# The first norm of a hybrid trunk step: its modulation by quarters of a channel, two column blocks ahead on rows 0 and 1, statistics in two parts

## The chip, the cores and the metric

One core of one Trainium2 chip runs the whole program. The metric is device time in microseconds, the median of three runs. The core has TensorE (PE, and PEld for its weight loads), VectorE (DVE), ScalarE (ACT), GpSimd (POOL) and SyncE (SP), whose queue issues most of the transfers.

## What is computed

One layer of a trunk on 640 tokens (128 of a prompt, 512 latent) of width 1024 in float32: a half-step SwiGLU feed-forward, a mixer, a second feed-forward, a last norm. The change touches only the first norm and the first products of the first feed-forward:

```python
mod = jax.nn.silu(cond) @ w_mod + b_mod              # cond: c or c_ctx
sh1, sc1, g1, shm, scm, gm, sh2, sc2, g2 = jnp.split(mod, N_MOD, axis=-1)
h = modulate(rmsnorm(x, norm_g[0]), sh1, sc1)        # h * (1 + sc1) + sh1
x = x + 0.5 * g1[:, None, :] * swiglu(h, ffn1_w1, ffn1_w2)
```

## The kernel before

Everything is kept transposed: 8 row tiles k of 128 features, 640 tokens in two halves h of 320. A product of float32 is made of three TensorE products of rounded parts (`three`, lines 245 to 247: hi by hi, lo by hi, hi by lo), 320 columns each; "a three" below is these. `split` (L75, L79) makes hi on ACT and lo on DVE, of weights (128x512, `wh`, `wl`) and of activations (128x320, `H..h`, `H..l`). The order of each engine's queue is that in which the program emits its instructions.

The stretch before the first full block goes so. SP issues ten loads of x (`x_load`), then the eight loads of channels SC1 and SH1 for rows 0 to 3 (the "upper" half, 512 KB each, `mod_load`: 2 KB packets), five into the ring `wr` and three into tiles `early`, then the weights of column blocks 0 and 1 for rows 0 to 3 (`two(0)`) and of block 2, then the eight loads for rows 4 to 7 ("low" units). Meanwhile `consts_in` makes silu of the conditioning (`cm`), `first(ch)` transposes a chunk of 128 tokens on PE, squares it on ACT with a sum along the row, and copies it out of PSUM (6 copies on DVE, 2 on ACT), `first_rows` makes the reciprocal norms of all five chunks (Sqrt, reciprocal, six diagonal matrices `dg`), and `rows_fn` spreads them by products with ones into two PSUM tiles (`N["rb", h]`). `scale_x` (L800) multiplies x by them.

A unit (L570) multiplies `cm` by one loaded tile: in `mod_half(.., wide=True)` two row tiles by 512 columns, so that four units make half a channel. Then `rows_` (L577) copies its PSUM rows, `turn` (L582) transposes them, and `put_` (L587, L589) sums four groups, adds the bias and writes `modT`. `gain` (L718, L719) makes the scale. `modulate` (L808 on ACT, L810 on DVE) applies scale and shift, and `first_put` splits the result into `H11` (h = 0, rows 0 to 3), `HT4` (h = 1, rows 0 to 3), `H21` and `H22` (rows 4 to 7).

`first_head` holds the first products: three column blocks t, halves h, rows k. For each h and each k of 0 to 3 it multiplies all three blocks, and between these it emits, by the table `then`, the low units, their rows, turns and puts, the remaining `scale_x` (`later`: eight of them), and the splits of the second half of the weights (`uncap`). Then `lower` modulates and splits rows 4 to 7, and k = 4 to 7 follow. PSUM comes from two pools of four banks, `big()` (`ps`) and `aux()` (`ax`).

POOL's queue loads channel G1 into the two tiles `mg` (`mod_own`); its first pair of loads waits for nothing but its place in the queue.

## Time and profile before

| what | us |
|---|---|
| median of 3 runs | 1672.75 (1672.16 to 1673.14) |
| the profiled execution, its own time | 1673.05 |
| its span, first to last instruction | 1671.3 |
| TensorE busy in the span | 1652.6 |
| VectorE busy | 1259.8 |
| ScalarE busy | 792.5 |

TensorE is busy in 99% of the span, and the granted clock is 1.00 in every slice. The page's 40 slices are 41.8 us each: only the first has TensorE at less than nine tenths, and the last one. A line of a timeline is one group of equal instructions of an engine, with its start, how long from the first start to the last end, and, in brackets, how long the engine had been idle and what ended that. A group's length is longer than the engine's step from one instruction to the next, because instructions overlap.

### The profile page before, as it was taken

What the parts mean: (1) busy time and instruction counts of PE and PEld (TensorE: products, weight loads), DVE (VectorE), ACT (ScalarE), POOL (GpSimd) and SP (SyncE); (2) the same over time, 40 slices, a digit from 0 to 9 for tenths busy, and PEclk for the clock granted to TensorE, in tenths of its full rate; (3) what the DMA queues carried; (4) which work ended last, traced back from release to release, by engine and by line L of the source; (5) the groups of instructions that cost most, each with busy time, mean ns of one, the idle gap of its engine ahead of it and who ended that gap; (6) DMA issues with size and microseconds to landing.
All of it is one profiled execution on the core that took longest, in us unless ns stands there. A gap on an engine that the chain in (4) does not pass through costs nothing.

```text
span 1671.3 us, 29257 instructions
## 1 busy us (share of the span) xinstructions
PE 1652.6 (99%) x11172; PEld 1607.3 (96%) x11172; DVE 1259.8 (75%) x2676; ACT 792.5 (47%) x1723; POOL 169.0 (10%) x251
## 2 busy tenths in 40 slices
PE   8999999999999999999999999999999999999998
PEld 4989999999999999999999999999999999999997
DVE  5867786887778778788897898779587467476576
ACT  5542452542565555455561455632375245254253
POOL 2010000000030321221121221011100000000002
PEclk9999999999999999999999999999999999999999
DMA  9344343343352533343258333457341322233221
GB/s 341 91 152 127 89 126 115 114 117 99 112 164 75 133 101 89 81 113 76 84 180 262 107 89 82 112 175 213 101 127 46 106 77 70 82 89 89 76 76 64
DMA packets 270972, 193.07 MB, mean 116 GB/s; under 512 B 8963, under 2 KB 247930, under 8 KB 270832
## 3 DMA queue, kind: packets, MB, share of 16 engines
q1 hardware_dynamic: 261248, 158.42, 32.6%
q0 software_dynamic: 9552, 32.77, 6.9%
q8 instruction: 88, 1.44, 0.4%
q14 instruction: 52, 0.43, 0.1%
q10 hardware_dynamic: 32, 0.01, 0.0%
HBM read 175.87 MB, written 15.31 MB: 114 GB/s over the span
## 4 chain that ended last, share of the span: by engine, by line
PE 93%; DMA 2%; ACT 2%; DVE 2%; issue 1%; SPq 0%; POOL 0%; ACTq 0%; DVEq 0%; POOLq 0%
PE ps L245 28%; PE ps L246 28%; PE ps L247 28%; PE ax L1460 2%; PE ax L1491 2%; PE ax L1463 1%; PE ax L570 1%; DMA wr<-in_w_mod_dram 1%; PE ax L1437 1%; DMA early<-in_w_mod_dram 0%; DMA wh<-in_x_sample_dram 0%; PE ax L661 0%; ACT Uh L808 0%; DMA wr<-in_w_ml_out_dram 0%; DVE wl L79 0%
## 5 line engine op out<-in xcount | busy, mean ns | idle before, releaser
L79 DVE TENSOR_TENSOR wl<-wr,wh 128x512 fp32r<-128x512 f32 (+1 forms) x408 | 267.1, 669 | 80.8 <-ACT wh L75 78.8
L75 ACT CAST wh<-wr 128x512 fp32r<-128x512 f32 (+1 forms) x410 | 239.1, 595 | 155.7 <-PE ps L246 136.6
L79 DVE TENSOR_TENSOR wl<-ws,wh 128x512 fp32r<-128x512 f32 x288 | 202.5, 703 | 44.9 <-ACT wh L75 44.1
L75 ACT CAST wh<-ws 128x512 fp32r<-128x512 f32 x288 | 176.1, 620 | 103.9 <-DVE ws L218 62.4
L245 PE MATMUL ps<-Uh,wh 128*128 128x320 f32 x704 | 218.8, 311 | 0.0
L246 PE MATMUL ps<-Ul,wh 128*128 128x320 f32 x704 | 217.2, 309 | 0.0
L247 PE MATMUL ps<-Uh,wl 128*128 128x320 f32 x704 | 217.1, 308 | 0.0
L889 DVE SCALAR_TENSOR_TENSOR x<-ps,modT,x 128x128 f32<-128x128 f32 (+2 forms) x216 | 82.8, 434 | 113.9 <-PE ps L247 113.8
L245 PEld LDWEIGHTS ps<-Uh,wh 128*128 128x128 f32 x704 | 132.1, 188 | 1.2 <-issue 0.8
L246 PEld LDWEIGHTS ps<-Ul,wh 128*128 128x128 f32 x704 | 132.1, 188 | 0.2 <-DVE Ul L79 0.2
L247 PEld LDWEIGHTS ps<-Uh,wl 128*128 128x128 f32 x704 | 132.1, 188 | 0.0
L245 PE MATMUL ps<-H11h,wh 128*128 128x320 f32 x384 | 121.1, 315 | 0.0
L245 PE MATMUL ps<-HT4h,wh 128*128 128x320 f32 x384 | 120.9, 315 | 0.0
L245 PE MATMUL ps<-H21h,wh 128*128 128x320 f32 x384 | 120.3, 313 | 0.4 <-ACT H21h L75 0.4
L246 PE MATMUL ps<-H11l,wh 128*128 128x320 f32 x384 | 118.8, 309 | 0.1
L246 PE MATMUL ps<-H21l,wh 128*128 128x320 f32 x384 | 118.7, 309 | 0.1
L247 PE MATMUL ps<-HT4h,wl 128*128 128x320 f32 x384 | 118.6, 309 | 0.0
L247 PE MATMUL ps<-H11h,wl 128*128 128x320 f32 x384 | 118.6, 309 | 0.0
L246 PE MATMUL ps<-HT4l,wh 128*128 128x320 f32 x384 | 118.6, 309 | 0.0
L247 PE MATMUL ps<-H21h,wl 128*128 128x320 f32 x384 | 118.4, 308 | 0.0
L245 PE MATMUL ps<-H22h,wh 128*128 128x320 f32 x352 | 110.2, 313 | 0.0
L246 PE MATMUL ps<-H22l,wh 128*128 128x320 f32 x352 | 108.9, 309 | 0.2
(411 smaller groups left out, 4490.3 us busy)
## 6 DMA issues: line engine op xcount, KB each, us to landing
wr<-in_ffn_w_dram SPq DMA_DIRECT2D x86, 512.0 KB, 3.9
wr<-in_w_in_dram SPq DMA_DIRECT2D x72, 512.0 KB, 3.9
wr<-in_w_mod_dram SPq DMA_DIRECT2D x56, 512.0 KB, 4.3
wr<-in_ffn_w_dram SPq DMA_DIRECT2D x48, 384.0 KB, 3.5
wr<-in_ffn_w_dram SPq DMA_DIRECT2D x20, 256.0 KB, 3.3
mg<-in_w_mod_dram POOLq DMA_DIRECT2D x8, 512.0 KB, 5.3
early<-in_w_mod_dram SPq DMA_DIRECT2D x8, 512.0 KB, 9.4
wr<-in_w_ml_out_dram SPq DMA_DIRECT2D x8, 512.0 KB, 4.9
```

Of the source, the lines that this page charges most:

```text
L75: A.copy(hi, raw)
L79: V.tensor_sub(lo, raw, f32(hi))
L245: PE.matmul(ps, hi[:, ws], ah, start=start, stop=False, skip_group_check=True)
L246: PE.matmul(ps, hi[:, ws], al, start=False, stop=False, skip_group_check=True)
L247: PE.matmul(ps, lo[:, ws], ah, start=False, stop=stop, skip_group_check=True)
L570: PE.matmul(S["p"][g, c:c + n], cm[:, k, :], w[:, n * j:n * j + n], start=(k < 4), stop=(k >= 4), skip_group_check=True, tile_position=(0, ...
L889: V.scalar_tensor_tensor(X[m][:, o + a:o + b], ps[:, a:b], modT[:, g, m, cd:cd + 1], X[m][:, o + a:o + b], op0=OP.mult, op1=OP.add)
L1437: PE.matmul(p[:, :P], S["k", dt][:, sl], S["q", dt][:, sl], start=(dt == 0), stop=(dt == 1))
L1460: PE.matmul(p2[:, :DH + 1], S["q", dt][:, sl], S["C"][d][:, dt, :], start=(dt == 0), stop=(dt == 1))
L1463: PE.matmul(p1[:, :DH + 1], S["p", ch][:, d, :], PO["vt"][:, ch, :], start=True, stop=True)
L1491: PE.matmul(p[:, :DH + 1], kw[:, dt * P:(dt + 1) * P], PO["vt"][:, ch, :], start=True, stop=True)
```

## The change

- The upper units come as quarters of a channel (`mod_quarters`): a load is four row tiles by 256 columns (`quarter_load`, 1 KB packets), two units make two row tiles of one channel, and rows, turn and put are done for each quarter. The order is SC1 and SH1 for rows 0 and 1, then SC1 and SH1 for rows 2 and 3. All eight have tiles `early`; the low units come three in the ring (`RING`) and five in `early` tiles again.
- On SP the weights of blocks 0 and 1 are issued behind the first four quarters, block 2 behind the other four, then low units 0 to 2 and 3 to 6; low unit 7 is issued after the first weights of the second half (`two(4)`), which are issued as `two(0)` is split.
- Blocks 0 and 1 multiply rows 0 and 1 of both halves first; then follow the units of the second four quarters, block 2 on rows 0 and 1, and the rest in a new order (`products`, `go`).
- x's statistics come in two parts (`first_rows(0)` after three chunks, `first_rows(1)` after five), and the spread rows lie in `big()` tiles. `scale_x` of rows 2 and 3 moves into `first_head`, behind the splits of rows 0 and 1.
- A Sqrt of a constant stands first on ACT; the silu of `consts_in` comes behind both Sqrt of the statistics. ACT makes one of the eight copies of a chunk out of PSUM (chunks 0 to 2) or none, where it made two.
- POOL copies a column of `modT` (the last shift of SH1) into each `mg` tile ahead of its first load, which so waits for it.

```diff
--- before.py
+++ after.py
@@ -590,6 +590,43 @@
         loads = [(mod_load if wide else quarter_load)(ch, half, i) for i in range(4)]
         return [(loads[i], unit_(i)) for i in range(4)], [rows_, turn, put_]
+    def mod_quarters(ch, half):
+        S = {}
+        def unit_(i):
+            q = i // 2
+            def emit(w):
+                if i % 2 == 0:
+                    S["p", q] = aux()
+                for j in range(4):
+                    g = slice(32 * j, 32 * j + 32)
+                    PE.matmul(S["p", q][g, :256], cm[:, 4 * (i % 2) + j, :], w[:, 256 * j:256 * j + 256],
+                              start=(i % 2 == 0), stop=(i % 2 == 1), skip_group_check=True, tile_position=(0, g.start))
+            return emit
+        def steps(q):
+            def rows_():
+                S["r", q] = t3()
+                (A.copy if ch == SH1 else V.tensor_copy)(S["r", q][:, :256], S["p", q][:, :256])
+            def turn():
+                S["c", q] = aux()
+                for j in range(2):
+                    PE.transpose(S["c", q][:, j * P:j * P + P], S["r", q][:, j * P:j * P + P], ident)
+            def put_():
+                k0 = 4 * half + 2 * q
+                o = modT[:, ch, k0:k0 + 2, :]
+                b0 = ch * KT + k0
+                V.tensor_reduce(o, S["c", q][:, :256].rearrange("p (j g r) -> p j r g", j=2, g=4)[:, :, 0:2, :],
+                                axis=mybir.AxisListType.X, op=OP.add)
+                V.tensor_add(o, o, bmT[:, b0:b0 + 2, None].to_broadcast([P, 2, 2]))
+            return [rows_, turn, put_]
+        return [(quarter_load(ch, half, i), unit_(i)) for i in range(4)], [steps(0), steps(1)]
     def mod_own(ch):
@@ -602,6 +639,9 @@
         def load(*ii):
             for i in ii:
                 tiles[i] = PO["mg"].tile([P, 1024], F32, name="mg", bufs=2)
+                if i < 2:
+                    G.tensor_copy(tiles[i][:, 0:1], modT[:, SH1, KT - 1, 0:1])
                 us[i][0](tiles[i])
         def two(v, *more):
@@ -786,8 +826,8 @@
             out.append((dg, c1 - c0, dst))
         return out
-    def spread(dgs):
-        p = aux()
+    def spread(dgs, p=None):
+        p = p or aux()
         for dg, n, dst in dgs:
             PE.matmul(p[:, dst:dst + n], ones, dg[:, :n], start=True, stop=True)
         return p
@@ -981,16 +1021,20 @@
                     PE.transpose(p[:, k * P:(k + 1) * P], XI[ch, q][:, k * P:(k + 1) * P], ident)
                 A.activation(scr, XI[ch, q], AF.Square, accum_out=ssq[:, ch, q:q + 1])
                 for k in range(4):
-                    (A.copy if k == 3 else V.tensor_copy)(X[4 * q + k][:, sl], p[:, k * P:(k + 1) * P])
-            V.tensor_add(ss[:, ch:ch + 1], ssq[:, ch, 0:1], ssq[:, ch, 1:2])
+                    (A.copy if k == 3 and q == 1 and ch < 3 else V.tensor_copy)(X[4 * q + k][:, sl], p[:, k * P:(k + 1) * P])
         return f
-    def first_rows():
-        A.activation(ss, ss, AF.Sqrt, scale=1.0 / D, bias=eps)
-        V.reciprocal(ss, ss)
-        r = lambda ch: ss[:, ch:ch + 1]
-        N["dg", 0] = diags([(r(0), 0, P, 0), (r(1), 0, P, P), (r(2), 0, 64, 256)])
-        N["dg", 1] = diags([(r(2), 64, P, 0), (r(3), 0, P, 64), (r(4), 0, P, 192)])
+    def first_rows(h):
+        def f():
+            a, b = ((0, 3), (3, NCH))[h]
+            V.tensor_add(ss[:, a:b], ssq[:, a:b, 0], ssq[:, a:b, 1])
+            A.activation(ss[:, a:b], ss[:, a:b], AF.Sqrt, scale=1.0 / D, bias=eps)
+            V.reciprocal(ss[:, a:b], ss[:, a:b])
+            r = lambda ch: ss[:, ch:ch + 1]
+            N["dg", h] = diags([(r(2), 64, P, 0), (r(3), 0, P, 64), (r(4), 0, P, 192)] if h else
+                               [(r(0), 0, P, 0), (r(1), 0, P, P), (r(2), 0, 64, 256)])
+        return f
     def first_scale(h, k):
         return lambda: scale_x(h, k, N["rb", h])
@@ -1011,6 +1055,7 @@
     def first_head(blocks):
         units = LOW[0] + LOW[2]
         fsc, fsh = LOW[1], LOW[3]
         work = right_chain(0, SH1)[1]
@@ -1025,9 +1070,9 @@
                 for i, col0 in enumerate((0, DFF)):
                     half_rows(ffn1_w1, col0, k0)(t[:, 512 * i:512 * i + 512])
             return load
-        loads = [two(0), blocks[2][0]] + [u[0] for u in units[OWN:]] + [two(4)] + [b[0] for b in blocks[3:]]
+        loads = [two(0), blocks[2][0]] + [u[0] for u in units[:RING]] + [two(4)] + [b[0] for b in blocks[3:]]
         part = lambda t, c: {"raws": [t], "n": 512, "src": lambda o: rtile[o["base"] + t][:, c:c + 512]}
-        l2 = 2 + len(units) - OWN
+        l2 = 2 + RING
         ops_ = [part(0, 0), part(0, 512), part(1, 0), part(1, 512), part(l2, 0), part(l2, 512)]
         ops_ += [part(t, c) for t in range(l2 + 1, l2 + 4) for c in (0, 512)]
@@ -1035,10 +1080,10 @@
             el = first_el[0]
             def take(i):
-                if i < OWN:
+                if i >= RING:
                     units[i][1](EARLY_T["low", i])
                     return
-                n = el["base"] + 2 + i - OWN
+                n = el["base"] + 2 + i
                 units[i][1](raw(n))
                 rdone.add(n)
                 load_more()
@@ -1053,15 +1098,26 @@
             owed.pop(0)()
             modulate(0, 1, 0, SH1, "A")
             first_put(0, 1)
-            ptr["cap"] = 3
-            w = W0 + [[op()]]
-            first_mod(0, 2, 3)
-            first_put(0, 2, 3)
-            ptr["cap"] = 4
-            w[2].append(op())
-            right_ = [lambda: first_mod(1, 0, 1), lambda: first_put(1, 0, 1), lambda: first_mod(1, 2, 3),
-                      lambda: first_put(1, 2, 3)]
-            ps = {(t, h): aux() if (t, h) in ((2, 0), (2, 1)) else big() for h in range(2) for t in range(3)}
+            first_mod(1, 0, 1)
+            first_put(1, 0, 1)
+            for h in (0, 1):
+                for k in (2, 3):
+                    first_scale(h, k)()
+            w = W0 + [[]]
+            ps = {(t, h): big() for h in range(2) for t in range(2)}
+            def products(h, ks, ts=(0, 1, 2)):
+                for k in ks:
+                    for t in ts:
+                        three(ps[t, h][:, :HT], *w[t][0], k, plain_acts(k, h), k == 0, False)
+            def go(*fs):
+                for f in fs:
+                    f()
+            def third():
+                ptr["cap"] = 4
+                w[2].append(op())
             def uncap():
                 ptr["cap"] = 1 << 20
@@ -1071,16 +1127,27 @@
             def lower(h, *ks):
                 return [lambda: first_mod(h, *ks)] + [lambda k=k: first_put(h, k) for k in ks]
             unit_ = lambda *ii: [lambda i=i: take(i) for i in ii]
-            then = {0: unit_(0, 1), 1: unit_(2, 3) + [fsc[0]] + right_,
-                    2: [fsc[1], fsc[2], gain(0, SC1, 4, 4)] + later, 3: unit_(4, 5),
-                    4: unit_(6, 7) + [fsh[0], uncap], 5: [fsh[1], fsh[2]] + lower(0, 4, 5), 6: lower(0, 6, 7),
-                    7: lower(1, 4, 5)}
+            up_ = lambda *ii: [lambda i=i: up[i][1](EARLY_T["up", i]) for i in ii]
+            qsc, qsh = UPQ[0][1], UPQ[1][1]
+            products(0, (0, 1), (0, 1))
+            products(1, (0, 1), (0, 1))
+            go(*up_(4, 5), qsc[0], lambda: early_low(7), *up_(6, 7), qsh[0])
             for h in range(2):
-                for k in range(4):
-                    for t in range(3):
-                        three(ps[t, h][:, :HT], *w[t][0], k, plain_acts(k, h), k == 0, False)
-                    for f in then.get(4 * h + k, ()):
-                        f()
+                ps[2, h] = aux()
+            ptr["cap"] = 3
+            w[2].append(op())
+            products(0, (0, 1), (2,))
+            go(*qsc[1:], gain(0, SC1, 2, 2))
+            products(1, (0, 1), (2,))
+            go(*qsh[1:], *lower(0, 2, 3), *unit_(0, 1), *lower(1, 2, 3))
+            products(0, (2, 3))
+            go(*unit_(2, 3), fsc[0], *later, third)
+            products(1, (2,))
+            go(fsc[1], fsc[2], gain(0, SC1, 4, 4), *unit_(4, 5))
+            products(1, (3,), (0,))
+            go(*unit_(6, 7), fsh[0], uncap)
+            products(1, (3,), (1, 2))
+            go(fsh[1], fsh[2], *lower(0, 4, 5), *lower(0, 6, 7), *lower(1, 4, 5))
             for f in lower(1, 6, 7):
                 f()
             close_early()
@@ -1114,40 +1181,48 @@
-    OWN, EARLY_T = 5, {}
+    RING, EARLY_T = 3, {}
     LOW = (*mod_half(SC1, 1, True), *mod_half(SH1, 1, True))
-    (usc, fsc), (ush, fsh) = mod_half(SC1, 0, True), mod_half(SH1, 0, True)
-    up = usc + ush
+    UPQ = []
+    (usc, q_), (ush, q2_) = mod_quarters(SC1, 0), mod_quarters(SH1, 0)
+    up = usc[:2] + ush[:2] + usc[2:] + ush[2:]
+    UPQ += [q_, q2_]
     def early_load(key, i, load):
         EARLY_T[key, i] = t = early.tile([P, 1024], F32, name="early", bufs=8)
         load(t)
     def early_up():
-        load_more(5)
-        for i in range(5, 8):
+        for i in range(4):
             early_load("up", i, up[i][0])
-    def early_low():
-        for i in range(OWN):
+        load_more(1)
+        for i in range(4, 8):
+            early_load("up", i, up[i][0])
+        load_more(2 + RING)
+    def early_low(*ii):
+        for i in ii:
             early_load("low", i, (LOW[0] + LOW[2])[i][0])
     def close_early():
         early_x.close()
         PO["hq"] = ctx.enter_context(pool("hq", side="right"))
-    uel = [element([load], [], emit) if i < 5 else step(lambda i=i, emit=emit: emit(EARLY_T["up", i]))
-           for i, (load, emit) in enumerate(up)]
-    fsc, fsh = [step(f) for f in fsc], [step(f) for f in fsh]
+    uel = [step(lambda i=i: up[i][1](EARLY_T["up", i])) for i in range(4)]
+    qsc, qsh = [step(f) for f in UPQ[0][0]], [step(f) for f in UPQ[1][0]]
     for ch in range(NCH):
         x_load(ch)
-    prog = [step(early_up), step(consts_in)] + [step(first(ch)) for ch in range(NCH)]
+    sqrt_first = tp.tile([P, 1], F32, name="rstd", bufs=2)
+    A.activation(sqrt_first, eps, AF.Sqrt, bias=eps)
+    prog = [step(early_up)] + [step(first(ch)) for ch in range(3)] + [step(first_rows(0)), step(first(3))]
     W0, RBS = [], {}
-    def keep_rows():
-        for h in range(2):
+    def spread_rows(h):
+        def f():
+            N["rb", h] = spread(N["dg", h], big())
             RBS[h] = t3()
             A.copy(RBS[h], N["rb", h][:, :HT])
+        return f
     def first_weights():
@@ -1156,11 +1231,11 @@
         for t in range(2):
             W0.append([op()])
         ptr["owe"] = False
-    prog += [step(first_rows), uel[0], step(consts_in2), uel[1], uel[2], step(rows_fn(0)), step(rows_fn(1)),
-             step(early_low), step(keep_rows)]
-    sc_ = [step(first_scale(h, k)) for h in (0, 1) for k in range(4)]
-    prog += sc_[:4] + uel[3:4] + fsc[:1] + sc_[4:6] + uel[4:5] + fsc[1:] + [step(gain(0, SC1, 0, 4))] + sc_[6:8] + uel[5:8]
-    prog += fsh[:1] + [step(first_weights)] + fsh[1:]
+    prog += [step(spread_rows(0)), step(first(4)), step(first_rows(1)), step(consts_in)]
+    prog += [step(first_scale(0, k)) for k in range(2)] + [step(consts_in2), step(spread_rows(1))]
+    prog += [step(first_scale(1, k)) for k in range(2)] + uel[:2] + qsc[:1] + uel[2:]
+    prog += [step(lambda: early_low(3, 4, 5, 6))] + qsc[1:] + [step(gain(0, SC1, 0, 2))] + qsh[:1] + [step(first_weights)]
+    prog += qsh[1:]
     later = [lambda h=h, k=k: scale_x(h, k, RBS[h]) for h in (0, 1) for k in range(4, 8)]
     ptr["cap"] = 0
     head, els = ffn(ffn1_w1, ffn1_w2, G1, after_lists(1, SHM), first_head)
```

## Rows read from the trace of the kernel before

**Rows 1.** Busy times by stretch (columns: stretch, its length, busy us and count of PE, PEld, DVE, ACT, POOL, granted TensorE clock, DMA share, GB/s).

```profile
0.00:29.60 29.60, 23.25 (x113) 12.10 (x113) 15.97 (x68) 14.58 (x42) 8.67 (x23) 1.00 0.98 335
29.60:50.15 20.55, 18.89 (x112) 12.37 (x112) 13.68 (x37) 9.71 (x23) 0.00 (x0) 1.00 0.93 296
50.15:100.00 49.85, 49.35 (x330) 46.54 (x331) 40.38 (x85) 28.99 (x64) 2.84 (x4) 1.00 0.27 82
```

**Rows 2.** TensorE's timeline, 0 to 30 us (start us, us, engine, line, operation, output<-inputs, count, idle time before it and what ended that). L981 is the transposes of x, L570 a unit of a modulation channel, L582 the transposes of its rows, L1049 the twelve products with zeros, L245 the first product of a block.

```profile
9.72 1.06 PE L981 MATMUL ax<-ident,wl 128*128 128x128 f32 x4
...
13.53 0.66 PE L981 MATMUL ax<-ident,wl 128*128 128x128 f32 x4 [0.33 <-ACT ax L982]
14.35 1.05 PE L570 MATMUL ax<-wr,cm 128*32 128x512 f32 x4 [0.17 <-issue]
...
25.51 1.05 PE L570 MATMUL ax<-early,cm 128*32 128x512 f32 x4 [0.34 <-DMA early<-in_w_mod_dram]
27.09 0.84 PE L582 MATMUL ax<-ident,t 128*128 128x128 f32 x4 [0.53 <-DVE t L577]
27.77 1.79 PE L1049 MATMUL ps<-nrow 128*128 128x320 bf16 x12
29.59 0.41 PE L245 MATMUL ps<-H11h,wh 128*128 128x320 f32 x1
```

**Rows 3.** ScalarE's timeline, 0 to 90 us, same columns.

```profile
4.55 1.28 ACT L521 ACT_TABLE_LOAD   x1 [4.55 <-PE ax L520]
...
15.41 1.28 ACT L989 ACT_TABLE_LOAD   x1
16.70 0.30 ACT L989 ACTIVATE ss<-ss,eps 128x5 f32<-128x5 f32 x1
...
29.07 0.46 ACT L75 CAST H11h<-Ul 128x320 fp32r<-128x320 f32 x1 [0.59 <-DVE Ul L810]
29.44 0.93 ACT L808 ACTIVATE Uh<-Uh,modT,gcol 128x128 f32<-128x128 f32 x2
...
57.57 1.28 ACT L915 ACT_TABLE_LOAD   x1
```

**Rows 4.** VectorE's timeline, 0 to 90 us, same columns, first the stretch of the statistics and the first blocks.

```profile
13.58 1.32 DVE L984 COPY x<-ax 128x128 f32<-128x128 f32 x6
...
17.27 1.20 DVE L785 TENSOR_SCALAR dg<-ident,ss 128x128 f32<-128x128 f32 x6
...
20.33 0.49 DVE L800 TENSOR_TENSOR Ul<-x,ax 128x320 f32<-128x320 f32 x1 [1.44 <-ACT t L1150]
20.73 0.48 DVE L800 TENSOR_TENSOR Uh<-x,ax 128x320 f32<-128x320 f32 x1
...
28.40 0.64 DVE L810 TENSOR_SCALAR Ul<-Ul,gcol,modT 128x128 f32<-128x128 f32 x2
28.96 0.68 DVE L77 TENSOR_TENSOR wl<-wr,wh 128x512 fp32r<-128x512 f32 x1
29.57 0.49 DVE L79 TENSOR_TENSOR H11l<-Ul,H11h 128x320 fp32r<-128x320 f32 x1
```

**Rows 5.** What the transfers moved, by stretch (the columns of rows 1; the last two are the DMA share and GB/s). In 19 to 23 and 31 to 37 us the packets are rows of 2 KB, in 24.5 to 26.5 of 512 B, in 1222 to 1224 (a quarter load of channel GM or G2) of 1 KB; in 14.5 to 18.5 POOL's queue of `mg` moves too, and the row of the queues in that stretch follows (packets, MB, share of 16 engines).

```profile
0.00:10.00 10.00, 6.53 (x27) 4.90 (x28) 3.54 (x18) 4.64 (x14) 7.18 (x21) 1.00 0.80 254
...
10.50:14.50 4.00, 3.26 (x20) 2.13 (x20) 3.26 (x17) 3.80 (x15) 1.38 (x2) 1.00 1.05 390
...
24.50:26.50 2.00, 1.66 (x8) 0.14 (x4) 0.38 (x1) 0.00 (x0) 0.00 (x0) 1.00 1.16 299
31.00:37.00 6.00, 5.38 (x29) 2.39 (x28) 3.21 (x7) 2.56 (x6) 0.00 (x0) 1.00 1.05 389
1222.00:1224.00 2.00, 2.00 (x17) 2.00 (x16) 1.94 (x5) 2.00 (x6) 0.00 (x0) 1.00 1.08 381
...
q0 software_dynamic: 270, 1.03, 63.6%
```

**Rows 6.** TensorE's timeline again: two blocks of h = 1 with a pair of wide units between them, and, from the stretch 1190 to 1280 us, two quarter units in a row.

```profile
42.94 0.31 PE L247 MATMUL ax<-HT4h,wl 128*128 128x320 f32 x1
43.17 1.07 PE L570 MATMUL ax<-wr,cm 128*32 128x512 f32 x8
44.17 0.42 PE L245 MATMUL ps<-HT4h,wh 128*128 128x320 f32 x1
...
50.15 0.41 PE L245 MATMUL ps<-H21h,wh 128*128 128x320 f32 x1 [0.40 <-ACT H21h L75]
...
1219.22 1.07 PE L570 MATMUL ax<-wr,cm 128*32 128x256 f32 x16
```

**Rows 7.** VectorE's timeline, 45 to 51 us.

```profile
45.39 0.49 DVE L800 TENSOR_TENSOR Uh<-x,t 128x320 f32<-128x320 f32 x1
45.79 0.42 DVE L577 COPY t<-ax 128x256 f32<-128x256 f32 x1
```

**Rows 8.** ScalarE's timeline, 470 to 492 us: squares (L753) ahead of and behind the load of the table for Sqrt (L777).

```profile
472.95 1.28 ACT L777 ACT_TABLE_LOAD   x1
...
476.19 0.47 ACT L753 ACTIVATE t<-x 128x320 f32<-128x320 f32 x1 [0.97 <-DVE x L889]
```

**Rows 9.** POOL's queue, 0 to 130 us (start us, us that the issue took, and what it had waited for).

```profile
89.70 1.42 POOL L541 DMA_DIRECT2D mg<-in_w_mod_dram  x2 [77.82 <-PE ax L570]
```

## The prediction

> **What bounds the kernel now.** I read the busy times by stretch first. From 50.15 us to 100 TensorE is busy 49.35 of 49.85 us, in the two stretches before 23.25 of 29.60 and 18.89 of 20.55, at a granted clock of 1.00 [rows 1]. Behind 50.15 the program is TensorE's own work, some ten thousand products in a row, so the end moves as the first product on rows 4 to 7 moves, which stands at 50.15 [rows 6]. The change can only act ahead of it.
>
> Then the timelines, for what ends last there. To 25.5 us the loads do: the eighth upper unit starts at 25.51 as its load lands [rows 2]. Its rows, transposes and sum take to 28.4, modulation and split another 1.2, and the first product starts at 29.59 [rows 2, 4]. From there TensorE works through 24 threes, eight low units and two transposes; at the end it waits 0.40 us for the split of row 4 [rows 6]. That one hangs on a line of VectorE: the row copy of the last low pair starts at 45.79, although the pair had ended at 44.2, because eight `scale_x` stood before it, the last at 45.39 [rows 6, 7]. From this copy to the product at 50.15 it is 4.36 us, which the change leaves as it is.
>
> **Loads.** x is 2.62 MB; 254 GB/s to 10.0 and 390 after put its end at 10.5 [rows 5]. A unit (0.524 MB) then takes 1.35 us at 389 GB/s in 2 KB packets, 1.38 at 381 in 1 KB packets, weights 1.75 at 299 [rows 5]: quarters cost 8 x 0.03 = 0.24 us in all. From the last byte to the start of the product I take 1.7 us: x and eight units had moved 6.8 MB, with 1.05 MB for `mg` and 0.13 of small things, at about 23.8 by the same rates; the unit started at 25.51. So the fourth quarter lands at 10.5 + 5.5 + 1.7 = 17.7, the weights at 19.5, the eighth quarter at 25.0, block 2 at 26.7 and, with low units 0 to 6 (9.45) and `two(4)` (1.75) ahead of it, the last low unit at 39.3. Taking `mg` out of this stretch, where it held 63.6% of the engines for four microseconds [rows 5], gives 1.05/0.39 = 2.7 us. Its new place costs nothing: behind the waiting POOL copy stand only `mg` loads, the next of them at 89.70 [rows 9], and `mg` would land near 55.
>
> **Front, up to the first unit (+3.9 us).** ACT loses a 1.28 us load at its start and seven copies; the Sqrt table at the head needs nothing of x, and squares run behind a Sqrt load without a new one [rows 3, 8]. VectorE gets the seven copies at 0.21 each (1.32 for six [rows 4]), and stands while part one passes through ACT. Chunk 3's last transposes start at 9.72 and take 1.06 [rows 2]; three copies, a sum, Sqrt, reciprocal and three diagonals (half of 1.20 [rows 4]) end at 12.8. Only then come 16 copies of the last two chunks, 3.2 us, to 16.0. Sum, Sqrt and reciprocal 0.75, diagonals 0.65: 17.4. TensorE spreads them by 18.2. ACT's load for silu, 1.28, now follows the second Sqrt: 16.5 to 17.75, `cm` at 17.95. First unit: 18.2, against 14.35 [rows 2]. It no longer waits for a load.
>
> ScalarE: Activation LUTs of the Trainium skill, "What ACT_TABLE_LOAD costs", puts a switch at 1283 ns and a drain of about 1380 more. Here the load starts 0.01 us after the copy before it ended and Sqrt follows 1.29 after its start [rows 3], so the trace shows no drain. By the page `cm` would come 1.4 us later and the sum below would be +3.1; I go by the row, and keep a longer switch as rival E.
>
> **Shifts of rows 0 and 1 (6.0 us earlier).** Two quarter units in a row took 1.07, I take 1.2 with the gap [rows 6]: four end at 20.6. Row copy, two transposes, reduce and add: 22.4, against 28.4.
>
> **The first products.** VectorE's queue from 22.4, in steps of 0.56 (modulate), 0.60 (128x512), 0.40 (128x320) [rows 4]: modulate, weight part, H11 lo, weight part, (wait for ACT's modulate, 0.93, and split, 0.46 [rows 3]) H11 lo at 25.0, modulate, wait, two HT4 lo, four `scale_x`: 28.8. TensorE's four threes of h = 0 go from 23.6 to 26.3, held by these. For h = 1 there is a new wait: the four `ps` tiles take over the banks of the two zero products and then of the two spread rows, so I expect h = 1 to wait for the last reader of the latter, the moved `scale_x`. No such wait is in the trace. Bounds: none, and TensorE goes on at 26.3; or also h = 0, then both wait. I take h = 1, by the order of release. 28.1, then 28.9 for the second block; done at 30.2. Behind this wait stand all the rest of TensorE's queue.
>
> **Rest of the stretch.** Second four quarters (landed) 2 x 1.2: 32.6; row copy and split of block 2's weights on ACT: 33.5; its four threes, with a wait for lo and one transpose: 36.0; transposes, put: shifts of rows 2 and 3 at 37.0. Low pair 1.2 (a wide pair: 42.94 to 44.17 [rows 6]) lies under that; H11 of row 2 at 38.4, and TensorE stands 0.9 us. Six threes of 0.44: 41.4. Low pair: 42.6. Three threes and transposes: 44.5. Low pair: 45.7. A three, low pair: 47.3. On VectorE, meanwhile: row copy 42.5, eight `scale_x` to 46.0, weight part 0.6, put and gain 0.84: 47.5, then the row copy of the last pair, where before it was 45.79.
>
> **Sum.** 47.5 + 4.36 = 51.85 against 50.15: **+1.7 us**. The start is 6 us earlier; 2.4 us of units, 0.6 of transposes, the 1.9, 0.9, 0.9 and some 2 us of smaller waits above eat it. On the profiled execution (1673.05, 1.75 more than its span, 0.3 above the median) it gives 1674.75, on the median 1674.4.
>
> At nothing, with their cover: block 3's load is issued as the split of block 2's second half ends, near 46.6; landing by 51, or 54 if `mg` takes its 64%, ahead of its split near 57.5; past that, TensorE would stand from 62.9. The Silu load at 57.57 [rows 3] falls away, but TensorE did not wait on ACT there: 0 to -0.4. The shorter load queue ends seven microseconds before TensorE asks (39.3 against 46.1), so rates matter little.
>
> **Rivals.** *A, no bank wait, or a quicker front*: without the wait 1.7 less, 1672.7; with the front at 16.0 too (parts one and two not holding VectorE) 2.2 less again, 1670.5. For it: banks are not shown in the trace; against: the order of release. *B, bound by loads*: if TensorE reaches the last low pair as it lands, 39.3, a unit of 1.05 and 4.36 put the product near 45.0, 5.2 us less than 50.15: 1667.6. It would need VectorE's steps of the head to overlap, 6 us of waits gone; the queue order speaks against it. *C, slower*: the first products themselves take the spread banks. Then h = 0 starts at 28.1, all eight threes end 1.5 later, 1.8 with the gaps: +3.5, 1676.2, and later still with the front behind 18.2. It decides from the first `ps` tile: a product that waits for `scale_x`. *E*: the switch to silu takes longer than its row, by once more its 1.28 us at most: `cm`, and all behind it, +3.0, 1675.7. Against it: the 0.01 and 1.29 us of the row. *D*, that the change does not do what it says, is in A to C: the first quarters being multiplied no sooner than 18 is part of my sum.
>
> **How the numbers follow.** About 0.2% (3.35 us) can be told from no change. Forecast 0.48 (1673 to 1676, all same), E 0.02 (same), A 0.21 (same), B 0.11 (faster), C 0.18, of which 0.16 is over 0.2%, for late fronts. So faster 0.11, same 0.73, slower 0.16. The range leaves out B and the far end of C: 1670.2 (A's bottom) to 1677.4 (C and a front of one microsecond more).
>
> **What would show it.** First unit near 18.2 with VectorE busy through 16; `modT` near 22.4; h = 1's first product ended by `scale_x`; TensorE's waits of about 0.9 near 31 and 38; the last low pair's row copy right behind VectorE's own queue near 47.5; first product on row 4 near 51.9; nothing changed behind it. Wrong if TensorE is dense from 23 us on (B), if an upper unit still waits for its load, if block 3's weights come late, or if the first three waits (C).

## The result, and the profile after

The changed kernel takes **1677.03 us** (median of 14 runs, 1674.08 to 1680.00), the kernel before beside it 1672.66 (14 runs, 1671.85 to 1673.14): ratio 1.0027, 95% interval 1.0019 to 1.0034. It is 4.4 us slower, just over the 0.2% that can be told from no change, and it spreads over 6 us where the kernel before spreads over 1.3. The forecast was 1674.4 with 0.73 on no change; the time lies in the range, on the side that had 0.16.

The profiled execution took 1675.82 us with a span of 1674.0, against 1673.05 and 1671.3. First the busy times by stretch (columns as in [rows 1]), then stretches of 2 us about the two places where the granted clock isn't 1.00.

```profile
0.00:29.60 29.60, 22.22 (x130) 15.04 (x131) 19.03 (x77) 16.14 (x41) 7.07 (x21) 0.94 0.99 319
29.60:50.15 20.55, 16.49 (x128) 10.15 (x126) 11.95 (x36) 6.51 (x15) 0.19 (x1) 1.00 0.84 264
50.15:100.00 49.85, 48.44 (x316) 45.81 (x316) 39.26 (x84) 27.68 (x64) 3.42 (x5) 0.97 0.35 103
14.00:16.00 2.00, 0.49 (x4) 0.38 (x4) 1.63 (x11) 1.19 (x4) 0.00 (x0) 1.00 1.09 348
18.00:20.00 2.00, 2.00 (x24) 0.87 (x20) 0.70 (x2) 0.00 (x0) 0.00 (x0) 0.50 1.09 332
48.00:50.00 2.00, 0.16 (x2) 0.00 (x0) 1.71 (x5) 0.86 (x3) 0.12 (x1) 1.00 0.66 197
50.00:52.00 2.00, 0.82 (x2) 0.58 (x3) 1.33 (x5) 2.00 (x6) 1.35 (x4) 0.76 0.58 166
52.00:54.00 2.00, 2.00 (x8) 2.00 (x8) 1.48 (x5) 1.52 (x4) 0.71 (x1) 0.50 0.99 318
54.00:56.00 2.00, 2.00 (x14) 2.00 (x14) 1.48 (x5) 1.56 (x4) 0.00 (x0) 0.88 0.82 277
```

Before, all three stretches had a granted clock of 1.00 [rows 1]. Now TensorE stands for most of 14 to 16 and of 48 to 50 us, and behind each of these waits the clock goes from 1.00 (2.4 GHz) to 0.50 (1.2 GHz) and comes back. TensorE's timeline shows what that does (L606 is a quarter unit, L570 a wide one, L245 the first product of a three):

```profile
17.05 3.53 PE L606 MATMUL ax<-early,cm 128*32 128x256 f32 x32 [0.16 <-ACT cm L521]
27.78 0.38 PE L245 MATMUL ps<-HT4h,wh 128*128 128x320 f32 x1 [1.67 <-DVE Uh L840]
29.99 1.93 PE L606 MATMUL ax<-early,cm 128*32 128x256 f32 x32
32.93 0.41 PE L245 MATMUL ax<-H11h,wh 128*128 128x320 f32 x1 [1.01 <-ACT wh L75]
37.61 0.41 PE L245 MATMUL ps<-H11h,wh 128*128 128x320 f32 x1 [0.78 <-ACT H11h L75]
45.40 1.06 PE L570 MATMUL ax<-early,cm 128*32 128x512 f32 x8
47.37 0.79 PE L582 MATMUL ax<-ident,t 128*128 128x128 f32 x4
51.18 0.64 PE L245 MATMUL ps<-H21h,wh 128*128 128x320 f32 x1 [3.02 <-ACT H21h L75]
...
52.41 0.47 PE L245 MATMUL ps<-H21h,wh 128*128 128x320 f32 x1
52.67 0.47 PE L246 MATMUL ps<-H21l,wh 128*128 128x320 f32 x1
...
54.65 0.31 PE L245 MATMUL ps<-H21h,wh 128*128 128x320 f32 x1
54.80 0.31 PE L246 MATMUL ps<-H21l,wh 128*128 128x320 f32 x1
```

The same 32 products take 3.53 us at 17.05 and 1.93 at 29.99; a product of the threes on row 4 lasts 0.47 us until 54.3 and 0.31 from there; they overlap, so one starts every 0.26 us, then every 0.15. The first product on row 4 stands at 51.18 instead of 50.15 [rows 6]. VectorE's timeline shows why it waits 3.02 us there, and where the front was quicker than summed:

```profile
11.83 3.25 DVE L1024 COPY x<-ax 128x128 f32<-128x128 f32 x16
...
21.88 0.16 DVE L626 TENSOR_TENSOR modT<-modT,bmT 128x4 f32<-128x4 f32 x1
...
45.13 0.49 DVE L840 TENSOR_TENSOR Uh<-x,t 128x320 f32<-128x320 f32 x1
45.53 0.69 DVE L79 TENSOR_TENSOR wl<-wr,wh 128x512 fp32r<-128x512 f32 x1
...
46.84 0.42 DVE L577 COPY t<-ax 128x256 f32<-128x256 f32 x1
48.22 1.29 DVE L79 TENSOR_TENSOR wl<-wr,wh 128x512 fp32r<-128x512 f32 x2 [0.96 <-ACT wh L75]
49.43 0.18 DVE L587 TENSOR_REDUCE modT<-ax 128x8 f32<-128x32 f32 x1
```

The last pair's row copy is right behind VectorE's own queue (46.84), as forecast, and 4.34 us lie from it to the product, as before (4.36). In these stand two weight parts of 1.29 us, though the transposes had ended at 48.2. POOL holds `mg` until the last shift is written, and nobody waits for it:

```profile
49.88 0.19 POOL L644 COPY mg<-modT 128x1 f32<-128x1 f32 x1 [41.43 <-DVE modT L589]
50.41 0.77 POOL L541 DMA_DIRECT2D mg<-in_w_mod_dram  x1 [0.35 <-POOL mg L644]
```

**A sum that closes.** Behind row 4 TensorE is the bound, so a span should move by the shift of the first product on row 4 plus half of the time that TensorE then runs at half clock. Here: 51.18 - 50.15 = 1.03; a stretch of 2 us at granted clock c holds 4 x (1 - c) us at 0.50, so 50 to 56 us hold 4 x (0.24 + 0.50 + 0.12) = 3.44, of which 0.14 lie ahead of 51.18; 1.03 + 3.3/2 = 2.7. The span moved by 2.7. The Trainium skill, "TensorE: Matmul & The Clock Gate", section "HAM oscillation — how this bites in real kernels", reckons the same half of the throttled time as the price. This trace agrees: half of 3.3 us closes the sum.

### The profile page after: what moved, and what is told of

Read it like the earlier page. It is cut to its first block, busy times and chain, and to the rows that moved or that the text cites. A ratio compares the mean times of both kernels' runs of the same rounds, so it can differ in the third digit from the quotient of the medians.

```text
span 1674.0 us, 29322 instructions
## 1 busy us (share of the span) xinstructions
PE 1650.4 (99%) x11204; PEld 1609.3 (96%) x11204; DVE 1261.7 (75%) x2687; ACT 789.2 (47%) x1717; POOL 167.7 (10%) x253
## 4 chain that ended last, share of the span: by engine, by line
PE 92%; DVE 3%; ACT 3%; issue 1%; DMA 1%; POOL 0%; ACTq 0%; DVEq 0%; POOLq 0%
PE ps L245 28%; PE ps L246 28%; PE ps L247 28%; PE ax L1535 2%; PE ax L1566 2%; PE ax L1538 1%; ACT Uh L848 1%; PE ax L1512 1%; DVE wl L79 1%; ACT wh L75 0%; DVE Uh L840 0%; DVE x L929 0%; PE ax L570 0%; PE ax L606 0%; PE ax L701 0%
## 5 line engine op out<-in xcount | busy, mean ns | idle before, releaser
L245 PE MATMUL ps<-Uh,wh 128*128 128x320 f32 x704 | 218.7, 311 | 0.0
L245 PEld LDWEIGHTS ps<-Uh,wh 128*128 128x128 f32 x704 | 132.1, 188 | 1.2 <-issue 0.8
L245 PE MATMUL ps<-H21h,wh 128*128 128x320 f32 x384 | 120.8, 315 | 3.0 <-ACT H21h L75 3.0
L245 PE MATMUL ps<-HT4h,wh 128*128 128x320 f32 x384 | 121.1, 315 | 1.7 <-DVE Uh L840 1.7
L245 PE MATMUL ps<-H11h,wh 128*128 128x320 f32 x384 | 120.9, 315 | 0.9 <-ACT H11h L75 0.8
L245 PE MATMUL ps<-H22h,wh 128*128 128x320 f32 x352 | 110.3, 313 | 0.0
```

Of the source, the lines that this page charges most:

```text
L245: PE.matmul(ps, hi[:, ws], ah, start=start, stop=False, skip_group_check=True)
```

## Experiments

Theory 1 (clock): the change's order makes waits of TensorE behind which the clock falls, and that is the term missing from my sum. Theory 2 (queues): the order costs what its waits last, and the clock adds nothing much. All runs, each with the kernel before beside it (1672.35 to 1672.80; e1 to e4 share a chip, e5 to e8, and e9 to e11); "row 4" is the first product on row 4 in the profiled execution, "half" the us at 0.50 behind it, "sum" as above, "span" the span less 1671.3:

| run | median us (range, runs) | ratio, 95% interval | row 4 | half | sum | span |
|---|---|---|---|---|---|---|
| changed | 1677.03 (1674.08 to 1680.00, 14) | 1.0027, 1.0019 to 1.0034 | 51.18 | 3.3 | +2.7 | +2.7 |
| e10 changed, again | 1675.46 (1674.63 to 1677.20, 11) | 1.0017, 1.0008 to 1.0026 | 51.38 | 5.9 | +4.2 | +4.1 |
| e1 | 1672.95 (1671.83 to 1675.16, 11) | 1.0007, 0.9998 to 1.0016 | 49.43 | 0 | -0.7 | -1.2 |
| e2 | 1672.72 (1672.01 to 1673.54, 11) | 1.0003, 0.9994 to 1.0012 | 49.65 | 0 | -0.5 | -0.4 |
| e9 | 1676.18 (1674.08 to 1678.15, 11) | 1.0021, 1.0012 to 1.0030 | 51.35 | 3.4 | +2.9 | +3.1 |
| e3 | 1674.04 (1672.34 to 1675.37, 11) | 1.0009, 1.0000 to 1.0018 | 47.79 | 3.4 | -0.6 | -0.7 |
| e4 | 1669.90 (1669.42 to 1670.99, 11) | 0.9986, 0.9977 to 0.9994 | 47.27 | 0 | -2.9 | -3.4 |
| e5 | 1678.36 (1676.67 to 1679.82, 6) | 1.0034, 1.0022 to 1.0047 | 53.35 | 6.4 | +6.4 | +5.2 |
| e6 | 1676.57 (1675.76 to 1678.21, 9) | 1.0026, 1.0016 to 1.0036 | 54.30 | 0 | +4.2 | +3.6 |
| e7 | 1676.57 (1676.00 to 1677.31, 10) | 1.0025, 1.0016 to 1.0034 | 53.41 | 0 | +3.3 | +3.2 |
| e11 | 1677.16 (1676.22 to 1679.90, 6) | 1.0030, 1.0018 to 1.0042 | 54.33 | 6.4 | +7.4 | +6.8 |
| e8 | 1671.11 (1669.26 to 1672.17, 11) | 0.9991, 0.9982 to 1.0000 | 47.44 | 0 | -2.7 | -2.4 |
| e12 | 1669.26 (1668.90 to 1670.67, 11) | 0.9981, 0.9972 to 0.9990 | 46.29 | 0 | -3.9 | -4.0 |

The sum meets the span within 0.6 us in all but e5 (1.2). The last four columns are of one execution, which need not lie at the median: those of e1 and e3 were the fastest of their runs, those of e10 and e11 the slowest.

**e1: the wait ahead of row 4 filled with products of zeros.** `busy` issues them into a PSUM tile that nobody reads.

```diff
+    def busy(n, alloc):
+        def f():
+            z = alloc()
+            for _ in range(n):
+                PE.matmul(z[:, :HT], zero[:, :P], zero, start=True, stop=True)
+        return f
...
-            go(fsh[1], fsh[2], *lower(0, 4, 5), *lower(0, 6, 7), *lower(1, 4, 5))
+            go(fsh[1], fsh[2], busy(20, aux), *lower(0, 4, 5), *lower(0, 6, 7), *lower(1, 4, 5))
```

> The changed kernel with twenty bf16 products with zeros (128x320, 2.9 us at the 0.147 us of such a product) in TensorE's queue between the transposes of the last shift and the first product on row 4, where TensorE waited 3.02 us; nothing else. Theory (queue and clock): in the profile of the changed kernel the granted clock is 0.50 from 51 to 54 us, right behind that wait, and half of about 3.4 us of work is lost; with the wait filled the clock stays at 1.00 there, the first product on row 4 stays near 51.2, and the time falls by about 1.7, from 1677.0 to about 1675.3, with a smaller spread of the runs. Rival (transfers moved behind 50 us, the mg loads and block 3, hold TensorE or its reads): the stretch behind 51 us is as slow as it was, and the time stays at 1677 within 0.7.

TensorE's timeline of e1, the zeros (L1060) and the first product on row 4, then the stretch behind:

```profile
46.24 2.88 PE L1060 MATMUL ax<-nrow 128*128 128x320 bf16 x20
49.43 0.41 PE L245 MATMUL ps<-H21h,wh 128*128 128x320 f32 x1 [0.31 <-ACT H21h L75]
```
```profile
50.00:52.00 2.00, 2.00 (x14) 2.00 (x15) 1.47 (x5) 1.52 (x5) 0.73 (x1) 1.00 0.95 292
```

Work without any use, 2.9 us of it, makes the kernel 4.1 us faster than the changed kernel's first measurement and 2.5 faster than its repeat, e10 (3.9 and 2.2 with the kernel before beside each taken off, as the chips differ). Under theory 2 it should have gained nothing. It is more than the 1.7 I gave it. In the profiled execution the front didn't fall either, but that is not the zeros' doing: they come behind it, and in e3 and e5, which have none, it stayed at 1.00 too.

**e2: zeros in all the larger waits.** As e1, and four, six, ten, six and four zeros in the front, ahead of h = 1, of block 2 and of row 2.

> As the run with zeros ahead of row 4, and further zero products in the other waits of the changed kernel: 4 and 6 ahead of the spread of the second statistics (TensorE idle 0.66 and 1.06 us there), 10 between the products of h = 0 and h = 1 (idle 1.67), 6 ahead of block 2's first product (idle 1.01), 4 ahead of row 2 (idle 0.78). Theory: no stretch at 0.50 clock from 14 us on; the sixteen quarter products take 2.4 us and not 3.5, so the shift of rows 0 and 1 is written at about 21.0 and not 22.0, the first product on row 4 comes about 1.0 us earlier, near 50.2, and the time is about 1674.3, close to the kernel before plus one microsecond. Rival: the zeros stand in the way, or the clock falls anyway: 1676 or more.

1672.72, the narrowest spread of the changed order (1.5 us), clock 1.00 throughout its first 100 us. This is the changed order's time without the clock: that of the kernel before.

**e9 and e10: zeros in the front only; the changed kernel again.** e9, ten zeros near 14 and 15 us (the ends of the two changed lines):

```diff
-step(first_rows(1)), step(consts_in)]
+step(first_rows(1)), step(consts_in), step(busy(4, aux))]
-[step(consts_in2), step(spread_rows(1))]
+[step(consts_in2), step(busy(6, aux)), step(spread_rows(1))]
```

> The changed kernel with ten products of zeros on TensorE in the two waits ahead of the first quarter units (near 14 and 15 us) and nothing else; the wait of 3.0 us ahead of row 4 stays empty. If the fall of the clock in the front costs the 1.75 us by which the profiled execution of the changed kernel had its first product later (23.25 against 21.51), and does so in most executions: 1675.3, row 4 still followed by a stretch at 0.50. If the wait ahead of row 4 alone set the four microseconds: 1677.0, no difference to the changed kernel run beside it.

> The changed kernel as it is, again, on the same chip and beside the same runs as the two others of this call. If its fall from full speed belongs to the program: median 1676 to 1678, executions from 1674 to 1680, the slow ones with the lower mean clock. If it belonged to the chip of the first measurement: 1673 to 1674.5, and the zeros of the run with 20 of them ahead of row 4 gave back only 1 to 1.7 us.

e10 came out at 1675.46, 1.6 lower than the first measurement but 2.7 above the kernel before: the loss belongs to the program. It lies between the two ranges expected, so part of the first measurement's 4.4 may not. e9 gained nothing on it (1676.18). In its profiled execution the front stays at 1.00, and the clock falls behind the next wait instead, that for the bank. Stretches of e9, then its timeline:

```profile
28.00:30.00 2.00, 2.00 (x14) 1.44 (x16) 0.00 (x0) 0.00 (x0) 0.00 (x0) 0.50 1.05 386
30.00:32.00 2.00, 2.00 (x32) 0.77 (x23) 0.42 (x1) 0.00 (x0) 0.00 (x0) 0.76 1.05 385
```
```profile
26.38 0.39 PE L245 MATMUL ps<-HT4h,wh 128*128 128x320 f32 x1 [1.67 <-DVE Uh L840]
29.39 2.69 PE L606 MATMUL ax<-early,cm 128*32 128x256 f32 x32
...
51.35 0.57 PE L245 MATMUL ps<-H21h,wh 128*128 128x320 f32 x1 [3.02 <-ACT H21h L75]
```

So there are three places (front, bank wait, row 4), and an execution falls in some of them. One line each from the windows of e3, e5, and twice e11:

```profile
50.00:52.00 2.00, 2.00 (x9) 2.00 (x9) 1.48 (x4) 1.60 (x5) 0.00 (x0) 0.50 0.92 281
30.00:32.00 2.00, 2.00 (x12) 1.67 (x15) 0.00 (x0) 0.00 (x0) 0.00 (x0) 0.50 1.05 389
20.00:22.00 2.00, 2.00 (x21) 0.66 (x13) 0.42 (x1) 0.00 (x0) 0.00 (x0) 0.50 1.09 349
30.00:32.00 2.00, 1.97 (x8) 1.84 (x8) 0.10 (x1) 0.00 (x0) 0.00 (x0) 0.51 1.05 387
```

Over all profiles of the changed order, row 4's wait of 3.02 us is followed by 0.50 in all six that leave it (the changed kernel, e3, e5, e9, e10, e11), and in none of the four that fill or shorten it (e1, e2, e8, e12). The front's empty waits are followed by it in three of seven (the changed kernel, e10, e11; not e1, e3, e5, e8), the empty bank wait in three of six (e5, e9, e11; not the changed kernel, e1, e10). So e5 falls at the bank wait without zeros in the front: that e9's zeros moved the fall there isn't shown. In e10 the stretch behind row 4 is twice as long as in the changed kernel's first profile:

```profile
50.00:52.00 2.00, 0.62 (x2) 0.39 (x2) 1.29 (x5) 1.95 (x6) 1.46 (x3) 0.60 0.51 144
52.00:54.00 2.00, 2.00 (x9) 2.00 (x9) 1.48 (x5) 1.51 (x5) 0.73 (x1) 0.50 0.98 301
54.00:56.00 2.00, 2.00 (x9) 2.00 (x9) 1.48 (x4) 1.60 (x4) 0.00 (x0) 0.50 0.89 287
56.00:58.00 2.00, 2.00 (x12) 2.00 (x11) 1.48 (x5) 1.60 (x5) 0.00 (x0) 0.69 0.14 55
```

That can make the spread: by the sum, a stretch more, or one twice as long, costs 1.7 us (half of 3.4). The first measurement's 14 executions point the same way without a trace: the three at 1678.5 and above had mean clocks of 0.993 to 0.995, the two under 1675 of 0.997 and 0.998.

**e3: the moved `scale_x` reads the SBUF copy of the spread row.**

```diff
-                    first_scale(h, k)()
+                    scale_x(h, k, RBS[h])
```

> The changed kernel with one edit: the four scale_x of rows 2 and 3 read the copies of the spread rows that ACT keeps in SBUF, not the PSUM tiles. Theory: the first product of h = 1 waited 1.67 us for the second scale_x because the ps tiles of h = 1 take over the banks of the spread rows; with the edit it follows the last product of h = 0 near 26.1, all behind it in TensorE's queue moves up by 1.7 us, and the first product on row 4 comes at 49.5 to 50.0; the time falls by 1.2 to 1.7, to about 1675.5, the clock's loss behind row 4's wait remaining. Rival: the next wait (block 2's weights, ready when ACT splits them, or VectorE's own queue ahead of the last row copy) takes it back: less than 0.5 us.

```profile
24.26 0.41 PE L245 MATMUL ps<-HT4h,wh 128*128 128x320 f32 x1
...
47.79 0.41 PE L245 MATMUL ps<-H21h,wh 128*128 128x320 f32 x1 [3.02 <-ACT H21h L75]
```

In e3's timeline h = 1 goes on without a wait, where e1 (same clock in the front) stood 1.66 us and had it at 26.02. The wait for the bank is shown, and it was worth 1.64 us on row 4 (47.79 against 49.43). The clock still falls behind row 4's 3.02 us. The median is 1.4 below e10's and 3.0 below the first measurement's, where 1.2 to 1.7 was expected.

**e4: the kernel before with the late `mg` alone.**

```diff
                 tiles[i] = PO["mg"].tile([P, 1024], F32, name="mg", bufs=2)
+                if i < 2:
+                    G.tensor_copy(tiles[i][:, 0:1], modT[:, SH1, KT - 1, 0:1])
```

> The kernel before with one part of the change alone: the first two mg loads wait for the last shift of SH1. Theory: up to 25.5 us the kernel before waits for loads, of which the mg tiles hold 1.05 MB, 2.7 us at 0.39 MB per us; the eighth upper unit starts at 22.8 to 23.5 and not 25.5, the first product at about 27.2, the first product on row 4 at 47.5 to 48.5 and not 50.15, and the time is 1670.0 to 1671.0. Rival: VectorE's and ACT's queues hold the same points, and the time is that of before within 0.5.

1669.90, 2.55 us less than the kernel before. The eighth upper unit starts at 22.66 instead of 25.51 [rows 2], the product on row 4 at 47.27 (TensorE's timeline of e4):

```profile
22.66 1.05 PE L570 MATMUL ax<-early,cm 128*32 128x512 f32 x4 [0.18 <-DMA early<-in_w_mod_dram]
...
47.27 0.41 PE L245 MATMUL ps<-H21h,wh 128*128 128x320 f32 x1 [0.38 <-ACT H21h L75]
```

One of the change's parts is a gain of 2.6 us; all the others together lose it and 2.7 to 4.4 more.

**e5: the changed kernel with `mg` at its old place** (its lines taken out again).

> The changed kernel with mg's two loads at their old place, near 10.4 us, and all else as changed. By the sum (loads bound the front: 1.05 MB more ahead of the quarters is 2.7 us, and the kernel before with only the late mg gained 2.55 us) the quarters land up to 2.7 us later, first product and first product on row 4 come 1 to 2.7 us later: 1677.0 + 1 to 2.7, about 1678.8. Rival: the front is bound by x's statistics, the first unit finds its quarters landed, and later units have slack: nothing, 1677.0 within 0.6.

1678.36, 1.3 to 2.9 above the changed kernel; row 4 2.0 us later than in e10. Against e1, whose front stayed at 1.00 like e5's, the first product comes 2.5 us later (24.02, 21.51). The quarters now wait for their loads:

```profile
19.25 0.64 PE L606 MATMUL ax<-early,cm 128*32 128x256 f32 x8 [0.99 <-DMA early<-in_w_mod_dram]
20.71 0.64 PE L606 MATMUL ax<-early,cm 128*32 128x256 f32 x8 [0.83 <-DMA early<-in_w_mod_dram]
```

So in the changed order too the late `mg` is worth about 2 us (by six runs, whose interval overlaps that of the changed kernel), and with it the loads are just off the path.

**e6 and e7: the kernel before with a long wait, empty and filled.** Seven multiplies on VectorE, whose result nobody reads; in e7 also zeros on TensorE (ends of the changed lines).

```diff
+            def pad():
+                t = t3()
+                for _ in range(7):
+                    V.tensor_mul(t, RBS[0], RBS[0])
-gain(0, SC1, 4, 4)] + later,
+gain(0, SC1, 4, 4)] + later + [pad],
-5: [fsh[1], fsh[2]] + lower(0, 4, 5)      (e7 alone)
+5: [busy(22, aux), fsh[1], fsh[2]] + lower(0, 4, 5)
```

> The kernel before with seven useless multiplies of 0.40 us on VectorE behind its eight later scale_x, so that the last low pair's row copy comes 2.8 us later and TensorE stands 3.3 us instead of 0.5 in one place. Queue arithmetic alone: first product on row 4 at 50.15 + 2.8 = 52.95, time 1672.45 + 2.8 = 1675.25, spread as before. Theory (the clock falls behind a wait of three microseconds in many executions, and what follows runs at half speed for 3.4 us): 1.5 to 2 us more, 1676.7 to 1677.3, with a spread of 3 us and more, and a stretch at 0.50 behind the wait.

> As the kernel before with the seven multiplies, and 22 products of zeros on TensorE (2.9 us) ahead of the transposes that wait. Queue arithmetic and theory agree here: 1675.25, granted clock 1.00. The difference to the run without the zeros is the clock's price alone: by the theory 1.5 to 2 us, by queue arithmetic 0.

Both took 1676.57: here the clock cost nothing in the median, and theory 1 missed. It did fall in e6 (0.50 in 50 to 52 us), but behind the transposes (their wait was 4.06 us), where TensorE still has six threes to do before row 4. At full speed it would have waited for row 4's split after them (e7: 0.39 us, at 53.41); at half speed it ends there 0.9 us later:

```profile
49.62 1.11 PE L582 MATMUL ax<-ident,t 128*128 128x128 f32 x4 [4.06 <-DVE t L577]
...
54.30 0.31 PE L245 MATMUL ps<-H21h,wh 128*128 128x320 f32 x1
```

The stretch at half speed is 3.4 us, 1.7 of work; about half of that lies in time that TensorE would have stood, 0.9 stays on row 4 in this execution and 0.4 on its span. Why none of it is left in the median isn't shown. Nor was e7 at 1.00 throughout, which was expected of it: in its front, ahead of any zeros, the clock fell behind a wait for a load (0.67 in 18 to 20 us, 0.50 in 20 to 22):

```profile
18.03 1.33 PE L570 MATMUL ax<-wr,cm 128*32 128x512 f32 x4 [2.10 <-DMA wr<-in_w_mod_dram]
```

That fall cost nothing. The loads set the pace there, and the first product on row 0 stood at 29.43, against 29.58 in e6. Both medians are 4.05 above the kernel before where 2.8 was expected. Row 4 moved by 3.3 in e7 (the seven multiplies took 0.49 each, not 0.40), and so did its profiled execution (3.2); the other 0.8 is where the two profiled executions lie among their runs (the kernel before 0.5 above its median there, e7 0.3 below its own).

**e11: the seven copies back on ScalarE** (the start of the changed line).

```diff
-(A.copy if k == 3 and q == 1 and ch < 3 else V.tensor_copy)
+(A.copy if k == 3 else V.tensor_copy)
```

> The changed kernel with the seven copies of x's transposes that went from ScalarE to VectorE back on ScalarE. If VectorE's copies of the last two chunks set the front, as in the sum (four of 0.20 us fewer there): first unit 0.8 us earlier than 17.0, time 0.8 us less than the changed kernel run beside it. Rival: ScalarE, with its squares and two Sqrt, then is the last, first unit at 17.0 or later, time the same or up to 0.8 us more.

The rival: first unit at 18.37 where e10, on the same chip, had 18.06, and 1.7 us slower. Three falls of the clock stand in its profile: in the front, twice as long as e10's, behind the bank wait and behind row 4's. So how much of the 1.7 is ScalarE's isn't settled; the first unit shows 0.3 of it, and that the copies gain nothing there.

**e8 and e12: the changed kernel mended.** e8: e3's edit; the lower parts of blocks 0 and 1 behind the last reduce; ten zeros ahead of row 4.

```diff
-                ptr["cap"] = 1 << 20
+                ptr["cap"], ptr["owe"] = 1 << 20, True
...
+            low4 = lower(0, 4, 5)
+            go(low4[0], owed.pop(0), *low4[1:], *[owed.pop(0) for _ in range(len(owed))])
```

> The changed kernel with three repairs: the moved scale_x read the SBUF copy of the spread row (the bank wait goes, 1.7 us), the lower parts of blocks 0 and 1's second halves (two of 0.60 us) go behind the last reduce on VectorE instead of ahead of it, and ten products of zeros stand ahead of row 4. First product on row 4 at 47.8 - 1.2 = 46.6, less than 1 us of wait, clock 1.00 there: 1670.0, range 1669.3 to 1671.5 (the upper end if the clock falls in the front). Rival (the order itself costs more than its waits): row 4 not ahead of 47.3, 1670.5 to 1672.

1671.11, in both ranges; row 4 at 47.44, where the rival had it. But the front of this execution was 0.87 us later than e3's (first product 22.43 against 21.56), and from there to row 4 it takes 25.01 us where e3 takes 26.23: the 1.2 that the edit should gain. e12 has that, e9's zeros, and another order instead of zeros ahead of row 4:

```diff
+            go(*up_(4, 5), qsc[0], *later[:2], lambda: early_low(7), *up_(6, 7), qsh[0])
...
+            go(*later[2:5])
...
+            go(*qsh[1:], *lower(0, 2, 3), *unit_(0, 1), *lower(1, 2, 3), *later[5:])
+            products(0, (2, 3))
+            go(*unit_(2, 3), fsc[0], third, *unit_(4, 5, 6, 7), fsh[0], uncap)
+            products(1, (2,))
+            go(fsc[1], fsc[2], gain(0, SC1, 4, 4), fsh[1], fsh[2])
+            low4 = lower(0, 4, 5)
+            go(low4[0], owed.pop(0), *low4[1:], *[owed.pop(0) for _ in range(len(owed))])
+            products(1, (3,))
+            go(*lower(0, 6, 7), *lower(1, 4, 5))
```

> The changed kernel with the late mg, the quarters and rows 0 and 1 first, but with the waits taken out by order: the moved scale_x read the SBUF copy; the eight later scale_x stand in three gaps of VectorE (two, three, three) instead of ahead of the last row copies; the last two low pairs follow the one before at once; the transposes of both come ahead of row 3's last three threes, which then cover the sum, modulation and split of row 4; the lower parts of blocks 0 and 1 come behind that; ten zero products in the front's two waits. From the run with the copied spread row, first product on row 4 at 47.79: the last pair ends 2 us earlier and 0.6 of 3.0 us of wait stay: 45.5, no stretch at 0.50 behind it. Its span of 1670.6 less 2.3 and less 1.4 of half speed: 1666.9, time 1668.7, range 1668.0 to 1670.5. Rival (the quarters' 3.5 us of extra units and the late front are the price, not the waits): not below the 1669.9 that the kernel before has with the late mg alone.

```profile
39.52 0.42 DVE L577 COPY t<-ax 128x256 f32<-128x256 f32 x1 [0.51 <-PE ax L570]
...
41.88 0.42 DVE L577 COPY t<-ax 128x256 f32<-128x256 f32 x1 [0.28 <-PE ax L570]
```
```profile
46.29 0.42 PE L245 MATMUL ps<-H21h,wh 128*128 128x320 f32 x1 [0.75 <-ACT H21h L75]
```

1669.26, faster than the kernel before by 3.1 us and the fastest of all. On VectorE's timeline of e12 the row copies of the low units, the last at 41.88, now wait for TensorE, not for eight `scale_x`; on TensorE's, row 4 waits 0.75 us, and the clock is 1.00 in the whole first 100 us. Against e4 it is 0.6 lower, on another chip and with intervals that overlap: that it beats the late `mg` alone isn't shown. The quarters and the early rows, mended, are worth little or nothing beside that one part (e12's front was as late as e8's: first product 22.47).

## Why the prediction came out as it did

**The order of events was right, the end too low by 2.6 us, and two errors of opposite sign hid each other.** That the time lies in the range is luck: its upper end, 1677.4, stood on rival C, which did not happen.

- First unit 18.2, measured 17.05 (16.90 in e1): VectorE's sixteen copies take the 3.2 us of the sum, but start at 11.83, not 12.8. The silu table's load took its 1.28 us: rival E did not happen.
- Shifts at 22.4, measured 22.05; h = 0 23.6, measured 23.25. This looks close, but the 32 quarter products had 3.53 us instead of the 2.4 I took, for the clock. Without the fall (e1: 1.93) the first product stood at 21.51, 2.1 ahead of my sum.
- The bank wait of h = 1, taken without a row that shows one: 28.1, measured 27.78 with a releaser that is the moved `scale_x`, 1.67 us, and gone in e3. Of rival A the missing bank wait is out, but its quicker front came in part (1.1 us of the 2.2); C is out, since h = 0 did not wait.
- Block 2 at 33.5 (32.93); wait for row 2 0.9 at 38.4 (0.78 at 37.61); the last row copy 47.5 (46.84); row 4 51.85 (51.18). No unit waited for its load (B out; e5 shows how near).
- The late `mg`: 2.7 us in the sum, measured 2.55 in e4 and about 2 in e5, and nothing paid at its new place (TensorE has no wait from 58 to 100 us).
- The prediction's list of what eats the six microseconds adds to 8.7 where its own times need 7.7; the forecast goes by the times.

**The step that failed is "nothing changed behind it"**: the granted clock stood in no term. The sum had TensorE stand some 3 us ahead of row 4 (last pair done at 47.3, product at 51.85) and did not ask at what speed the products behind that wait would run. In the first profiled execution the clock took about 1.6 us in the front (the 32 products 3.53 against 1.93 in e1; first product 23.25 against 21.51, of which 0.15 is the first unit's) and 1.65 behind row 4. Without the first, row 4 stands at 49.4 to 49.7 (e1, e2), so my sum of queues was 2.2 to 2.4 us too late, and the change with the clock kept up is at 1672.72 (e2): no change. The clock took 2.7 to 4.3 us more in the median (e10, the first measurement). The chance of 0.16 for slower stood on C, which isn't what happened.

What stays open: when the front and the bank wait fall and how long a stretch lasts; row 4's wait fell in every profile that left it. One execution of each kernel was profiled. The 1.6 us between the two measurements of the changed kernel aren't explained either; in the profiles of this order the products that spread the second rows start anywhere from 15.84 (e1) to 16.75 us (e8), with no zeros ahead of them.

## What to carry to other kernels

Where TensorE bounds what follows, a wait has two prices: its length, and, where the granted clock goes down behind it, half of the time at 1.2 GHz; look for the longest waits just ahead of dense work, and cover them by order first and by useless products if nothing else is there. A fall that meets slack costs less (e6) or nothing (the front of e7). And measure the parts of a bundled change one at a time: here two lines were worth 2.6 us, and all the rest lost it.

## What the runs showed of the hardware that I had not expected

- Twenty useless products (2.88 us on TensorE) made a kernel 2.5 to 4.1 us faster (2.2 to 3.9 with the kernel before beside each taken off).
- A wait of 3.02 us ahead of the same work was followed by 3.4 us at 0.50 in one execution and by 6.8 in another of the same program, and such a kernel spreads over 6 us where the kernel before spreads over 1.3: the spread can itself be a sign.
- The same wait of 1.67 us was followed by a stretch at 0.50 in the profiles of e5, e9 and e11 and stayed at 1.00 in the changed kernel's two and e1's: the length of a wait alone does not say whether the clock falls behind it.
